# A hybrid decoder step: the first feed-forward slice by four plain products, tiles turned in another order

## The chip, the cores and the metric

The kernel runs on one core of one Trainium2 chip. The metric is device time in microseconds (us) of one execution. The engines are PE (TensorE matmuls), ACT (ScalarE), DVE (VectorE), POOL (GpSimd) and SP, which issues most DMAs.

## What is computed

One layer of a decoder for 1024 prompt tokens and 64 sample tokens (8 sequences of 8), all in float32:

```python
h = h + concat([o_gla, o_mla]) @ w_o                # (1024+64) x 1024
n = rmsnorm(h, g_ffn)
a, c = n @ ffn_w_gate, n @ ffn_w_up                 # 1024 -> 2816 each
conv = b + sum(w[j] * full[:, j:j + T] for j in range(3))   # causal, full = prev + a
h = h + (silu(conv) * c) @ ffn_w_down
h = h + (p @ ple_w_proj) * sigmoid(rmsnorm(h, g_ple) @ ple_w_gate)
```

`o_gla` is gated linear attention, `o_mla` multi-head latent attention; for the sample tokens the latter goes over a paged cache of 8192 past positions for each sequence.

## The kernel before, in words

Every float32 operand of a matmul is split into a high part (a cast on ACT) and a low part (the difference, on DVE or POOL; `split`, lines 114 to 117). A product is three matmuls: high by high, high by low, low by high (`mm3`, lines 138 to 141). The compiler's list scheduler orders the instructions of each engine; the program's text gives the priority, `keep_in_program_order` and `issue_after` hold single instructions back. `issue_after(x)` sets the instructions of its block that run on x's engine behind x. Engines then run their queues in order.

**Stages.** Dense projections and prompt attention run first, together with the cache stream: 64 blocks of the paged cache (`cache_stream`), each scored, softmaxed (`stage_b`, `stage_c1`) and multiplied (`stage_pv`, L646). When the dense work has ended, the stream runs on with the output projection as filler: `wo_units` is a generator of 65 units, of which unit 1 loads operands. Six passes over channel pairs make units 2 to 49; the last 16 units (channels 6 and 7) go tile by tile, two halves of 512 columns for each 128-row tile, in the order `order = (6, 7, 0, 3, 1, 4, 2, 5)`. Each adds its PSUM result to the residual rows (L1441). When a tile has both halves, `normed` makes its row sums (L1467 on ACT, L1468 and L1469 on POOL), copies the rows to DRAM (L1599), and normalises them in place (`xnorm`): by one DVE operation (L1476), or, for the tiles whose bit is set in `VIAP`, by ACT and then POOL (L1478, L1479). VIAP = 20 picks tiles 2 and 4. `fill(n)` draws n units; the last blocks of the stream draw 1, 3, 2, 1, 5 and 4.

**Hand-over.** Then come, in the text's order: tiles 6 and 7 turned for the "rest" (`turned_rest`: 8 transpositions, L132, and two splits each), three calls of `turned_pair`, the sample rows' share of `w_o` (`down_sample`, with weights `w45` of channels 4 and 5 loaded through the staging rooms `stg`, of which there are three), and `normed` and `turned_rest` of the sample rows.

**Slices.** The feed-forward goes in 22 slices of 128 columns (`ff_chunk`). Tokens 0 to 767 are two halves of NP = 384 columns, inputs are two halves of 512 features, so gate and up of a slice are a 2 by 2 block product. It is made with seven products (Winograd's form): with input blocks 11, 21 (tokens 0 to 383) and 12, 22 (tokens 384 to 767), `turned_pair(t)` turns tiles t and t + 3 and forms

```python
t1 = x12 - x11;  t2 = x22 - t1;  t3 = t2 - x11;  t4 = x21 - t2
```

in the rooms of the rows themselves (`quarter`), and splits 11, 21, 22, t1 to t4 (`put`). `ff_weights(f)` loads four weight blocks g0, g1, u0, u1 (L1713), forms four sums s1 to s4 on POOL (L1720 to L1726) and splits eight blocks into a ring of rooms (`wroom`, NWB = 10: four in pool `fw`, six in `fv`). A product is 12 matmuls of 384 columns. The remaining 256 prompt and 64 sample columns (NR = 320) are the "rest": 24 plain matmuls for gate and 24 for up. Slice 0 does its gate rest late, behind the turned sample rows; the others do it after the first two products.

**Rooms.** SBUF pools are opened on two sides like stacks; a room opened where another was waits, tile by tile, for the last use of what lay there. Decode constants and block rooms are in `cp` on the right. `wo_room` lays out on the left, in turn, `hp` (the eight row tiles, 6 and 7 first, and the gain), `wq`, `fb`, `wf`, `ct`, `sg`. After the stream, `xhl` (turned blocks) takes the right side, then `xh2`, `fw`, `fv`; `tp` (slice buffers) takes the left side.

**PSUM.** There are eight banks: pools pd (3), pm (2), and, after the stream, p2t (2) and p2 (1). `both` deals them out in turn to the products.

After the slices come the down projection, the per-layer embedding and the outputs.

Of the kernel before, what the change touches and what calls it, by code (L numbers as in the profile page):

```python
# [18 lines left out]
P = 128  # L19
D = 1024  # L20
# [9 lines left out]
PLAN = ([0], [], [1, 2, 3])  # L30
VIAP = 20
GS0 = 1
# [12 lines left out]
def step_kernel(ctx: ExitStack, tc: tile.TileContext, A):  # L45
# [561 lines left out]
    def stage_c1(o):  # L607

        nt = o.nt
        sb = o.sn[:, :nt, :]  # L610
        mt = pm([P, 512], "mt")
        drain = o.n - NB * 8 + 3
        if drain == 1:
            fill(49 - z["units"])
        elif drain == 2:
            fill(2)
        pe.transpose(mt[:, 0:P], o.ml.rearrange("p a c -> p (a c)"), ident)
        m = cp.tile([P, 1], F32, tag="bm", name="bm", bufs=4)
# [11 lines left out]
        act.copy(phl[:, :nt, 0:64], sb)  # L630
        pool.tensor_tensor(phl[:, :nt, 64:128], sb, phl[:, :nt, 0:64].bitcast(F32), ALU.subtract)  # L631
# [25 lines left out]
    def stage_c2(o):  # L657
# [14 lines left out]
        dve.tensor_scalar(ol, ol, rl, None, ALU.mult)  # L672
        if b == NB - 1:
            fill(4)
        pt = pm([P, 512], "pt_ol")
# [847 lines left out]
    room = {}  # L1523
    order = (6, 7, 0, 3, 1, 4, 2, 5)

    def wo_room():
# [5 lines left out]
        z["late"], z["WvT"] = (z["fb"].tile([P, n], F32, name=nm) for nm, n in (("late", 648), ("WvT", 512)))  # L1532
        room["wf"] = opened("wf", 2)
        room["ct"] = opened("ct")
        room["sg"] = opened("sg")

    def wo_units():
# [3 lines left out]
        for g in range(3):  # L1541
# [98 lines left out]

    tw = opened("tw")
    w45 = [wload(z["tw"], A["w_o"][0][c * P:(c + 1) * P, :], 1, D, "w45", 2, 3, stg) for c in (4, 5)]

    NP = 384
    NR = T - 2 * NP + R
    rx = opened("xhl", side="right")  # L1650
    xb = {nm: [z["xhl"].tile([P, 4, NP], F32R, name=f"x{nm}{s}") for s in "hl"] for nm in ("t2", "t1", "22", "21", "11")}
    xr = [z["xhl"].tile([P, 8, NR], F32R, name=f"xr{s}") for s in "hl"]

    def turned_rest(t):
# [9 lines left out]

    def turned_pair(t):

        pt = {}
        for nm, bank, rows, k0 in (("11", p2t, t, 0), ("12", pd, t + 3, 0), ("22", pd, t + 3, 4), ("21", p2t, t, 4)):
            pt[nm] = bank([P, 4, P], "pt")
            for k in range(4):  # L1670
                pe.transpose(pt[nm][:, k], hrows(rows)[:, (k0 + k) * P:(k0 + k + 1) * P], ident)
        b11, t1, t2, t3 = quarter(t, 0), quarter(t, 1), quarter(t + 3, 0), quarter(t + 3, 1)
        act.copy(b11, pt["11"])
        dve.tensor_tensor(t1, pt["12"], b11, ALU.subtract)
        dve.tensor_tensor(t2, pt["22"], t1, ALU.subtract)
# [3 lines left out]
        pool.tensor_tensor(t3, t2, b11, ALU.subtract)
# [15 lines left out]
    def wroom():  # L1695

        i = ring[0] % NWB
        ring[0] += 1
        where, n = (z["fw"], 4) if i < 4 else (z["fv"], NWB - 4)
        return [where.tile([P, 4, P], F32R, tag="w" + s, name="w" + s, bufs=n) for s in "hl"]  # L1700
# [60 lines left out]
    def ff_chunk(f):  # L1761
# [105 lines left out]
    for t in range(3):
        turned_pair(t)
    for f in range(2):
        down_sample([(z["oTm"][:, c], [w[:, 0, f * 512:f * 512 + 512] for w in w45[c]]) for c in (0, 1)] +  # L1870
                    [(z["oTm"][:, c - 4], wow[c, f]) for c in (6, 7)], pm, f, f == 0)
# [3 lines left out]
    rx2 = opened("xh2", side="right")
    xb.update({nm: [z["xh2"].tile([P, 4, NP], F32R, name=f"x{nm}{s}") for s in "hl"] for nm in ("t4", "t3")})
    for t in range(3):
        last_sums(t)
    normed(NT)
    room["hp"].close()  # L1880
# [9 lines left out]
    rt.close()  # L1890
    fv.close()
    fw.close()
    rx2.close()
    rx.close()

# [367 lines left out]
```

## Time and profile before

| what | value |
|---|---|
| runs, us | 2217.87, 2218.1, 2211.19 (median 2217.87) |
| span of the profiled execution, us | 2211.1 |
| PE busy, us (matmuls) | 2126.7 (13460) |
| DVE busy, us | 1668.4 |
| ACT busy, us | 1366.7 |
| POOL busy, us | 1233.9 |
| mean granted clock of PE | 0.988 |

The span runs from the first to the last instruction of one execution; the runs are timed by themselves and lie between 0.1 and 7.0 us above it. In a line of the order in time, the columns are start, duration, engine, source line, operation, what it writes and reads, shape and number of merged instructions; in brackets stands the idle time ahead of it and what ended it. In a list of groups, busy time and mean duration in ns follow the count. "L139" is line 139 of the program, often one of a helper, so the tile's name tells more.

### The profile page before, as it was taken

How to read it: one execution, taken by the hardware profiler on the slowest of the kernel's cores; microseconds unless marked ns; L12 is line 12 of the kernel's file. 1: busy time of each engine (PE TensorE's matmuls, PEld its weight loads, DVE VectorE, ACT ScalarE, POOL GpSimd, SP SyncE). 2: the span in 40 equal slices, each digit the busy share in tenths (PEclk: the TensorE clock that was granted, in tenths of full speed). 3: DMA queues.
4: the chain of work that ended last, by engine and by line, in shares of the span. 5: the costliest groups of instructions: out<-in, count | busy, mean ns of one | idle time of the engine just before them, and what ended most of it. 6: DMA issues, size and time to landing. Idle time of an engine off the chain costs nothing.

```text
span 2211.1 us, 38379 instructions
## 1 busy us (share of the span) xinstructions
PE 2126.7 (96%) x13460; PEld 1927.2 (87%) x13460; DVE 1668.4 (75%) x2551; ACT 1366.7 (62%) x3724; POOL 1233.9 (56%) x1330
## 2 busy tenths in 40 slices
PE   7999989999999999999999997999999999999999
PEld 6889978878888888887898875999999999888899
DVE  4775667467788888887888788888888886887642
ACT  5676766777778888887777766333333333534631
POOL 5675668576777777778455557756566562011100
PEclk9999999999999999999999998999999999999999
DMA  5343235412342222221522222332232325777321
GB/s 185 106 144 108 78 119 156 141 54 69 105 120 61 63 74 61 61 56 46 171 77 69 74 77 82 101 102 90 92 95 91 101 91 191 240 218 237 101 71 39
DMA packets 204418, 233.07 MB, mean 105 GB/s; under 512 B 42422, under 2 KB 146339, under 8 KB 204227
## 3 DMA queue, kind: packets, MB, share of 16 engines
q1 hardware_dynamic: 188259, 179.49, 26.0%
q0 software_dynamic: 14736, 46.67, 7.4%
q10 hardware_dynamic: 1232, 4.46, 0.5%
q8 instruction: 108, 1.77, 0.3%
q14 instruction: 83, 0.68, 0.1%
HBM read 188.00 MB, written 42.52 MB: 104 GB/s over the span
## 4 chain that ended last, share of the span: by engine, by line
PE 79%; DVE 7%; ACT 5%; DMA 3%; POOL 3%; issue 2%; SPq 0%; DVEq 0%; POOLq 0%; ACTq 0%
PE ps_gu L140 7%; PE ps_gu L141 7%; PE ps_gu L139 7%; PE ks L139 5%; PE ks L141 4%; PE ks L140 4%; PE ps_dn L140 3%; PE ps_dn L141 3%; PE ps_dn L139 3%; PE cpv L646 2%; PE ctp L522 2%; PE ps_lt L278 2%; PE ps_pj L139 2%; DVE css L565 1%; PE ps_pj L140 1%
## 5 line engine op out<-in xcount | busy, mean ns | idle before, releaser
L560 ACT ACTIVATE csq<-ks 128x256 f32<-128x256 f32 x1040 | 392.7, 400 | 91.1 <-PE ks L141 80.2
L565 DVE TENSOR_REDUCE css<-csq 128x16 f32<-128x1024 f32 (+1 forms) x264 | 315.7, 1196 | 61.2 <-ACT csq L560 58.2
L115 ACT CAST wh<-st 128x512 fp32r<-128x512 f32 x176 | 108.4, 619 | 189.0 <-PE ps_gu L140 168.7
L139 PE MATMUL ks<-mv0h,cTh 128*128 128x320 f32 (+1 forms) x520 | 171.0, 331 | 8.8 <-ACT sn L562 4.6
L139 PE MATMUL ks<-mv1h,cTh 128*128 128x320 f32 (+1 forms) x520 | 169.6, 328 | 7.8 <-ACT sn L562 3.5
L605 POOL TENSOR_TENSOR chl<-craw,chl 128x1024 fp32r<-128x1024 f32 x64 | 141.6, 2213 | 55.2 <-ACT chl L603 53.0
L140 PE MATMUL ks<-mv1l,cTh 128*128 128x320 f32 (+1 forms) x520 | 153.1, 296 | 0.0
L140 PE MATMUL ks<-mv0l,cTh 128*128 128x320 f32 (+1 forms) x520 | 152.0, 294 | 0.0
L141 PE MATMUL ks<-mv0h,cTl 128*128 128x320 f32 (+1 forms) x520 | 147.6, 297 | 0.9 <-DVE cTl L116 0.8
L141 PE MATMUL ks<-mv1h,cTl 128*128 128x320 f32 (+1 forms) x520 | 148.0, 298 | 0.1
L116 DVE TENSOR_TENSOR wl<-st,wh 128x512 fp32r<-128x512 f32 x132 | 119.0, 903 | 26.3 <-ACT wh L115 26.3
L631 POOL TENSOR_TENSOR phl<-sn,phl 128x512 fp32r<-128x512 f32 (+1 forms) x64 | 85.5, 1335 | 84.8 <-ACT phl L630 84.3
L116 POOL TENSOR_TENSOR wl<-st,wh 128x512 fp32r<-128x512 f32 x44 | 69.4, 1578 | 102.9 <-ACT wh L115 102.9
L140 PE MATMUL ps_dn<-o 128*128 128x512 f32 x308 | 120.1, 390 | 0.4 <-DVE o L116 0.4
L141 PE MATMUL ps_dn<-o 128*128 128x512 f32 x308 | 120.2, 390 | 0.0
L116 DVE TENSOR_TENSOR cTl<-ctp,cTh 128x512 fp32r<-128x512 f32 (+1 forms) x136 | 90.0, 662 | 37.8 <-ACT cTh L115 36.8
L139 PEld LDWEIGHTS ks<-mv0h,cTh 128*128 128x128 f32 x520 | 97.9, 188 | 23.2 <-ACT sn L562 9.4
L562 ACT COPY sn<-ks 128x64 f32<-128x64 f32 x520 | 116.7, 224 | 0.0
L139 PEld LDWEIGHTS ks<-mv1h,cTh 128*128 128x128 f32 x520 | 99.0, 190 | 20.1 <-ACT sn L562 7.9
L1318 POOL TENSOR_TENSOR pl<-p,ph 128x512 fp32r<-128x512 f32 (+1 forms) x96 | 97.5, 1020 | 30.3 <-DVE ph L1317 21.2
L139 PE MATMUL ps_dn<-o 128*128 128x512 f32 x308 | 112.1, 390 | 0.0
L141 PE MATMUL ps_gu<-xrh,wl 128*128 128x320 f32 x352 | 108.7, 309 | 0.0
(670 smaller groups left out, 7871.4 us busy)
## 6 DMA issues: line engine op xcount, KB each, us to landing
raw<-ds SPq DMA_DIRECT2D x77, 256.0 KB
raw<-ffn_w_down SPq DMA_DIRECT2D x66, 256.0 KB
stage<-w_in SPq DMA_DIRECT2D x48, 256.0 KB
st<-ffn_w_gate SPq DMA_DIRECT2D x44, 256.0 KB
st<-ffn_w_up SPq DMA_DIRECT2D x44, 256.0 KB
wr<-ffn_w_down SPq DMA_DIRECT2D x44, 256.0 KB
ds<-cv SPq DMA_DIRECT2D x21, 512.0 KB
oraw<-doT SPq DMA_DIRECT2D x16, 256.0 KB
```

What stands on the lines that cost most here:

```text
L115: cast = act.copy(hi, src)
L116: res = (lo_eng or dve).tensor_tensor(lo, src, hi.bitcast(F32), ALU.subtract)
L139: pe.matmul(ps, ah, bh, start=first, stop=False)
L140: pe.matmul(ps, ah, bl, start=False, stop=False)
L141: return pe.matmul(ps, al, bh, start=False, stop=last)
L278: pe.matmul(ps, x, w, start=first, stop=last)
L560: act.activation(sq[:, f * 256:f * 256 + 256], ks[:, 0:256], AF.Square)
L562: act.copy(o.sn[:, g0 + i, :], ks[:, 256:320])
L565: dve.tensor_reduce(o.ss[:, g0 + i + 1 - n:g0 + i + 1, :].rearrange("p i h -> p (i h)"), sq2[:, :n].rearrange("p i (h n) -> p (i h) n", n= ...
L605: pool.tensor_tensor(ch[:, c0:c1, 128:256], src, ch[:, c0:c1, 0:128].bitcast(F32), ALU.subtract)
L631: pool.tensor_tensor(phl[:, :nt, 64:128], sb, phl[:, :nt, 0:64].bitcast(F32), ALU.subtract)
L1318: pool.tensor_tensor(pl[:, c0:], p[:, c0:], ph[:, c0:].bitcast(F32), ALU.subtract)
```

## The change

The first slice is computed by four plain products of 24 matmuls each (`plain`: gate and up for both halves of tokens), which need blocks 11, 21, 12, 22 and the four plain weight blocks only. Its elementwise part is a function of its own (`first_chunk`). The weights of slice 0 are loaded and split through the staging rooms `stg` with `ff_weights(0)`, whose ACT casts are set behind the last block's softmax cast (`z["phl"]`), into a new pool `fr` on the right side. The last 16 projection units go in tile order 0 to 7; the last four of them are no longer drawn by the stream's last block (`fill(4)` is gone) but drawn among the calls that turn tiles 0 to 5 (`turned_tile`). The sums t1 and t2 still come from turning, t3, t4 and the splits of t1 to t4 in `sums` and a `put` around the last plain products. VIAP = 85 picks tiles 0, 2, 4 and 6 for ACT and POOL. Rows are laid as 6, 7, 3, 4, 5, 0, 1, 2, `sg` below `ct`, `ct` is closed before `xhl`, and `tp`'s rooms in another order. The `w45` weights go to rooms of `wf` in place of a pool of their own. Slices 1 to 21 are computed as before.

```diff
-VIAP = 20
+VIAP = 85
...
-        act.copy(phl[:, :nt, 0:64], sb)
+        z["phl"] = act.copy(phl[:, :nt, 0:64], sb)
...
-        if b == NB - 1:
-            fill(4)
...
-    order = (6, 7, 0, 3, 1, 4, 2, 5)
+    order = (6, 7, 3, 4, 5, 0, 1, 2)
...
-        for t in order:
+        for t in range(NT):
             for f in range(2):
                 wo_unit((6, 7), t, f)
...
-    def turned_pair(t):
+    def turned_tile(t):
+        n, rest = t % 3, t > 2
+        raw = []
+        for i, nm in enumerate(("12", "22") if rest else ("11", "21")):
+            pt = (pd, p2t)[i]([P, 4, P], "pt")
             for k in range(4):
+                pe.transpose(pt[:, k], hrows(t)[:, (4 * i + k) * P:(4 * i + k + 1) * P], ident)
+            put(n, nm, pt, dve)
+            raw.append(pt)
+        b11, b21 = quarter(n, 0), quarter(n, 1)
+        if not rest:
+            act.copy(b11, raw[0])
+            act.copy(b21, raw[1])
+        else:
+            t1, t2 = quarter(t, 0), quarter(t, 1)
+            dve.tensor_tensor(t1, raw[0], b11, ALU.subtract)
+            dve.tensor_tensor(t2, raw[1], t1, ALU.subtract)
+    def sums(n):
+        b11, b21, t1, t2 = quarter(n, 0), quarter(n, 1), quarter(n + 3, 0), quarter(n + 3, 1)
+        put(n, "t2", t2, dve)
+        pool.tensor_tensor(b11, t2, b11, ALU.subtract)
+        put(n, "t1", t1, pool)
+        pool.tensor_tensor(b21, b21, t2, ALU.subtract)
+        put(n, "t3", b11, pool)
...
+    def plain(key, ws, xs):
+        ps = early[key] = both([P, 512], "ps_gu")
+        for i, (wn, xn) in enumerate(zip(ws, xs)):
+            for k in range(4):
+                mm3(ps[:, :NP], wgu[0][wn][0][:, k], wgu[0][wn][1][:, k], xb[xn][0][:, k], xb[xn][1][:, k],
+                    i == k == 0, i == 1 and k == 3)
...
+    unit = lambda: next(z["fill"], done) is None
+    with tc.issue_after(z["phl"].ins):
+        ff_weights(0)
+    for w in (0, 1, unit, 2, unit, unit, 3, unit, 4, 5):
+        w() if w is unit else turned_tile(w)
...
+    plain("g1", ("g0", "g1"), ("11", "21"))
+    for f in range(2):
+        down_sample([(z["oTm"][:, c - 4], wow[c, f]) for c in (6, 7)] +
+                    [(z["oTm"][:, c], w45[2 * c + f]) for c in (0, 1)], pm, f, f == 0)
+    plain("u1", ("u0", "u1"), ("11", "21"))
     turned_rest(6)
     turned_rest(7)
...
+    normed(NT)
+    plain("g2", ("g0", "g1"), ("12", "22"))
+    for n in range(3):
+        sums(n)
+    plain("u2", ("u0", "u1"), ("12", "22"))
...
+    for n in range(3):
+        put(n, "t4", quarter(n, 1), dve)
+    turned_rest(NT)
```

More of the change, by code (lines that the diff above doesn't have):

```diff
@@ L1533, in wo_room @@
         room["wf"] = opened("wf", 2)
+        room["sg"] = opened("sg")
         room["ct"] = opened("ct")
-        room["sg"] = opened("sg")
     def wo_units():
@@ L1639, in both @@
         return (pd, pm, pd, pm, pd, p2)[turn[0]](shape, name)
-    tw = opened("tw")
-    w45 = [wload(z["tw"], A["w_o"][0][c * P:(c + 1) * P, :], 1, D, "w45", 2, 3, stg) for c in (4, 5)]
     NP = 384
     NR = T - 2 * NP + R
+    room["ct"].close()
     rx = opened("xhl", side="right")
-    xb = {nm: [z["xhl"].tile([P, 4, NP], F32R, name=f"x{nm}{s}") for s in "hl"] for nm in ("t2", "t1", "22", "21", "11")}
+    xb = {nm: [z["xhl"].tile([P, 4, NP], F32R, tag=f"x{nm}{s}", name=f"x{nm}{s}") for s in "hl"]
+          for nm in ("t2", "22", "11", "21", "t1", "12")}
     xr = [z["xhl"].tile([P, 8, NR], F32R, name=f"xr{s}") for s in "hl"]
+    fr = opened("fr", side="right")
     def turned_rest(t):
@@ L1698, in wroom @@
         ring[0] += 1
-        where, n = (z["fw"], 4) if i < 4 else (z["fv"], NWB - 4)
+        where, n = (z["fr"], 4) if i < 4 else (z["fv"], NWB - 4)
         return [where.tile([P, 4, P], F32R, tag="w" + s, name="w" + s, bufs=n) for s in "hl"]
@@ L1708, in ff_weights @@
         fs = slice(f * P, (f + 1) * P)
-        raw, hl = [], wroom()
+        raw, hl = [], wroom() if f else None
         for nm in ("ffn_w_gate", "ffn_w_up"):
             for i in range(2):
-                r = wstage()
+                r = wstage() if f else stg([P, 512], F32).rearrange("p (k c) -> p k c", c=P)
                 sp.dma_start(r, A[nm][0][i * 512:(i + 1) * 512, fs].rearrange("(k p) c -> p k c", p=P))
                 raw.append(r)
+        w = wgu[f] = {}
+        if not f:
+            for nm, r, eng in zip(("g0", "g1", "u0", "u1"), raw, (pool, pool, dve, dve)):
+                w[nm] = block(r, eng)
+            return
         g0, g1, u0, u1 = raw
         s1, s2 = wstage(), wstage()
-        w = wgu[f] = {}
         w["g0"] = block(g0, dve, hl)
@@ L1782, in ff_chunk @@
         pool.tensor_copy(a_s[:, :, 0:2], prv[:, f])
+        if not f:
+            return first_chunk(w, a, a_s, cv, cvs, conv, w3)
         m1, m2 = product("g0", "11"), product("g1", "21")
@@ L1791, in gate_rest @@
             act.copy(a_s[:, :, 2:10], pg[:, T - 2 * NP:NR].rearrange("p (b t) -> p b t", t=8))
-        if f:
-            gate_rest()
+        gate_rest()
         if f + 1 < NF:
@@ L1847, in ff_chunk @@
         dve.tensor_tensor(v, m4, v, ALU.add)
-        if not f:
-            turned_rest(NT)
-            gate_rest()
         if not last:
@@ new lines, in step_kernel @@
+    unit = lambda: next(z["fill"], done) is None
[3 more added lines that the diff above has]
+        w() if w is unit else turned_tile(w)
+    for _ in z["fill"]:
+        raise AssertionError
+    w45 = []
+    for c in (4, 5):
+        for f in range(2):
+            hl = [z["wf"].tile([P, 512], F32R, tag=f"s{f}{k}", name=f"s{k}", bufs=2) for k in "hl"]
+            raw = stg([P, 512], F32)
+            sp.dma_start(raw, A["w_o"][0][c * P:(c + 1) * P, f * 512:f * 512 + 512])
+            split(*hl, raw)
+            w45.append(hl)
@@ L1865, in step_kernel @@
+    plain("g1", ("g0", "g1"), ("11", "21"))
+    for f in range(2):
+        down_sample([(z["oTm"][:, c - 4], wow[c, f]) for c in (6, 7)] +
+                    [(z["oTm"][:, c], w45[2 * c + f]) for c in (0, 1)], pm, f, f == 0)
+    plain("u1", ("u0", "u1"), ("11", "21"))
     turned_rest(6)
     turned_rest(7)
[L1867 to L1871, printed above, removed]
@@ L1872, in step_kernel @@
-    tw.close()
-    for nm in ("sg", "ct", "wf", "fb", "wq"):
-        room[nm].close()
[L1875 to L1880, printed above, removed]
+    room["sg"].close()
+    room["wf"].close()
+    rx2 = opened("xh2", side="right")
+    xb["t3"] = [z["xh2"].tile([P, 4, NP], F32R, name=f"xt3{s}") for s in "hl"]
+    normed(NT)
@@ L1889, in step_kernel @@
         sample_rows(late[0], half)
[L1890 to L1894, printed above, removed]
+    for r in (rt, fv, fw, rx2, fr, rx):
+        r.close()
     NK = NF // 2
```

53 lines of the change are left out of this document (32 added, 21 removed).

## The prediction

> **What bounds the kernel now.** I read the page first, then the busy time by stage, then who waited for whom, and last the matmuls in order of time across the hand-over from the decode stream to the feed-forward slices.
>
> ```profile
> span 2211.1 us, 38379 instructions
> ```
> ```profile
> 1300.20:1323.30 23.10, 21.54 (x108) 17.36 (x107) 19.39 (x29) 13.72 (x34) 15.94 (x19) 1.00 0.28 114
> 1323.30:1359.89 36.59, 22.34 (x115) 16.64 (x114) 31.84 (x47) 27.23 (x56) 25.73 (x20) 0.83 0.28 87
> 1359.89:1395.67 35.78, 33.58 (x189) 31.50 (x189) 29.86 (x35) 15.88 (x30) 28.96 (x26) 0.93 0.32 89
> 1395.67:1860.00 464.33, 464.33 (x2799) 460.65 (x2798) 388.31 (x519) 177.16 (x348) 272.19 (x261) 1.00 0.29 95
> ```
>
> The columns are length, then busy time of PE, PEld, DVE, ACT and POOL, then granted clock. From 1395.67 to the end of the slices PE is busy all the time at full clock. So whatever brings the matmul stream forward before 1395.67 shortens the kernel by as much, and nothing behind that point changes. The loss sits in 1323.30 to 1359.89, where PE is busy 22 of 37 us and even that at a clock of 0.83.
>
> ```profile
> PE ps_gu L139 <- ACT wh L115: 6.4, 1, 6.4
> PE pt L1671 <- DVE h L1674: 2.3, 2, 1.7
> PE pt L1671 <- DVE x22l L116: 2.1, 1, 2.1
> ```
>
> The first slice's matmuls wait 6.4 us for its weight cast on ScalarE; the transpositions of paired tiles (L1671) wait again and again for the subtraction that frees a PSUM bank.
>
> **The matmul ledger of before.** I take the stretch from the first matmul of the last four projection units to the point at which slice 0 is finished and slice 1 has done its two gate products and its gate rest.
>
> ```profile
> 1313.90 1.03 PE L132 MATMUL pt<-ident,h 128*128 128x128 f32 x8
> 1323.30 0.39 PE L1434 MATMUL ps_dn<-wdh,sh 128*128 128x512 f32 x1
> 1328.65 0.39 PE L1438 MATMUL ps_dn<-wdh,sl 128*128 128x512 f32 x1
> 1333.02 1.15 PE L717 MATMUL po_mla<-oTm,WvT 128*64 128x64 f32 x16
> 1351.49 0.39 PE L1447 MATMUL ps_ds<-w45h,oTm 128*128 128x512 f32 x1
> 1353.11 0.39 PE L1450 MATMUL ps_ds<-wdl,oTm 128*128 128x512 f32 x1
> 1359.89 0.69 PE L139 MATMUL ps_gu<-x11h,wh 128*128 128x384 f32 x1 [6.39 <-ACT wh L115]
> 1362.51 0.52 PE L139 MATMUL ps_gu<-x11h,wh 128*128 128x384 f32 x1
> 1364.75 0.39 PE L140 MATMUL ps_gu<-x11l,wh 128*128 128x384 f32 x1
> 1376.47 0.33 PE L139 MATMUL ps_gu<-xt4h,wh 128*128 128x384 f32 x1
> 1378.38 0.34 PE L141 MATMUL ps_gu<-xt4h,wl 128*128 128x384 f32 x1
> 1378.65 0.71 PE L132 MATMUL pt<-ident,hs 64*128 64x64 f32 x8
> 1380.46 0.41 PE L139 MATMUL ps_gu<-x21h,wh 128*128 128x384 f32 x1 [1.10 <-DVE a L1811]
> 1393.03 0.31 PE L139 MATMUL ps_gu<-xrh,wh 128*128 128x320 f32 x1
> 1395.52 0.31 PE L141 MATMUL ps_gu<-xrh,wl 128*128 128x320 f32 x1
> 1395.67 0.34 PE L139 MATMUL ps_gu<-xt2h,wh 128*128 128x384 f32 x1
> ```
>
> Matmuls overlap, so the price of one is the distance between starts. 24 projection matmuls from 1323.30 to 1328.65: 5.35/23 = 0.2326 us. 8 sample matmuls from 1351.49 to 1353.11: 1.62/7 = 0.231. Twelve products of 384 columns from 1376.47 to 1378.38: 1.91/11 = 0.1736. Eighteen of 320 columns from 1393.03 to 1395.52: 2.49/17 = 0.1465. Work between 1323.30 and 1395.67:
> 24 projection 5.6; seven tiles to turn, 7 x 1.03 = 7.2 (the eighth, tile 6, was turned in the gap at 1313.90); sample rows 0.7; the decode output 1.2; 16 sample matmuls 3.7; slice 0: seven products of 12, 84 x 0.1736 = 14.6, and two rests of 24, 48 x 0.1465 = 7.0; slice 1: 24 x 0.1736 = 4.2 and 24 x 0.1465 = 3.5. Sum 47.7. The stretch lasts 1395.67 - 1323.30 = 72.4, so 24.7 us are lost.
>
> **The change, part by part.** *Plain products.* Slice 0 takes four products of 24 matmuls in place of seven of 12: 96 for 84, 12 x 0.1736 = 2.1 us more on PE, all on the path. In return nothing of t1 to t4 and no s1 to s4 is needed before PE may start slice 0.
> *Turning.* Eight turned tiles as before; 7.2 to 8.2 us in the stretch, by whether the gap at 1313.90 takes tile 0. I take 7.7. PE work after: 47.7 + 2.1 + 0.5 = 50.3. With no loss at all the gain is 72.4 - 50.3 = 22.1 us.
> *Tile order and normalisation.* Tiles go 0 to 7, and VIAP moves tiles 0, 2, 4, 6 to ScalarE and GpSimd where only 2 and 4 were.
>
> ```profile
> L1476 DVE SCALAR_TENSOR_TENSOR h<-h,rs,gb 128x1024 f32<-128x1024 f32 x6 | 8.7, 1451 | 1.5 <-DMA dhp<-h 1.5
> L1479 POOL TENSOR_TENSOR h<-h,gb 128x1024 f32<-128x1024 f32 x2 | 4.7, 2364 | 3.5 <-ACT h L1478 3.5
> L1478 ACT ACTIVATE h<-h,rs 128x1024 f32<-128x1024 f32 x2 | 2.3, 1151 | 0.2 <-POOL rs L1469 0.2
> 1318.54 1.30 POOL L631 TENSOR_TENSOR phl<-sn,phl 128x512 fp32r<-128x512 f32 x1 [1.91 <-ACT phl L630]
> 1322.33 1.12 PE L646 MATMUL cpv<-chl,phl 128*128 128x258 f32 x8
> ```
>
> DVE sheds 2 x 1.45, ACT gains 2 x 1.15, POOL gains 2 x 2.36. On POOL one such norm may now stand ahead of the last softmax split (L631). That ends at 1319.84 and its matmuls start at 1322.33, behind projection units: a slack of 2.5 us covers a norm of 2.36. I cost it at 0; without the cover, 2.4.
> *Weights of slice 0.* Their casts go right behind the last softmax cast on ACT, with three staging rooms.
>
> ```profile
> 1282.81 5.34 SPq L157 DMA_DIRECT2D stg<-w_o  x3
> 1326.76 0.33 SPq L157 DMA_DIRECT2D stg<-w_o  x1
> 1373.29 3.76 DMA st<-ffn_w_up
> ```
>
> Before, the same three rooms took three w_o loads at 1282.81, 44 us before the fourth, which got its room at 1326.76. In the new order the weights of slice 0 stand in those places: three lie ready, the fourth lands at about 1326.8 + 3.8 = 1331. So the 6.4 us wait goes. What is late next is the turned tiles.
>
> *Loss 1, the tiles.* These are the rows for the vector work:
>
> ```profile
> L1441 DVE TENSOR_TENSOR h<-h,ps_dn 128x512 f32<-128x512 f32 x16 | 10.7, 679 | 3.0 <-PE ps_dn L1438 3.0
> L116 DVE TENSOR_TENSOR x21l<-pt,x21h 128x512 fp32r<-128x512 f32 x3 | 2.0, 677 | 0.0
> L116 DVE TENSOR_TENSOR xt4l<-h,xt4h 128x512 fp32r<-128x512 f32 x3 | 4.7, 1620 | 0.4 <-ACT xt4h L115 0.4
> L116 POOL TENSOR_TENSOR xt3l<-h,xt3h 128x512 fp32r<-128x512 f32 x3 | 4.6, 1571 | 2.7 <-ACT xt3h L115 2.7
> L1679 POOL TENSOR_TENSOR h<-h,h 128x512 f32<-128x512 f32 x3 | 4.2, 1390 | 0.9 <-DVE h L1675 0.9
> 1336.74 1.29 DVE L1476 SCALAR_TENSOR_TENSOR h<-h,rs,gb 128x1024 f32<-128x1024 f32 x1 [1.52 <-DMA dhp<-h]
> ```
>
> From 1323.30 DVE still has 4 additions of 0.68, one norm of 1.45, 6 splits of tiles 0 to 2 and 12 operations of tiles 3 to 5 at 0.68, and the low halves of u0 and u1 at 0.68: 2.7 + 1.45 + 4.1 + 8.2 + 1.4 = 17.9, to 1341. Two tiles turned earlier take off 2.7, and the first product needs tile 5's banks, not its last subtractions, another 1.4 or more: 1336 to 1340. PE's own work before its first plain product is 5.6 + 1.2 + 5 or 6 tiles, so 1335 to 1336. I take 3.5 lost; 1 if DVE keeps up, 8 if every norm waits for the copy of its row to DRAM as at 1336.74.
> *Loss 2, the clock.* At 1362.51 to 1364.75 the products ran 2.24/7 = 0.32 us apart, not 0.1736, after the idle stretch. The new stretch has shorter gaps: 1 us, bounds 0 and 2.4 (as before: 16 products slow by 0.146).
> *Loss 3, slice 1.* Its staging rooms open behind those of the projection and the rows; a load costs 3.76 to land, then GpSimd's four subtractions of 1.39 and the splits. PE has the sample matmuls, u1, g2, u2 and two rests meanwhile. 2 us, bounds 0 and 6.
> *Loss 4, sample rows.* They need both sample sums, a row norm and a turn before the rests, as at 1380.46 (1.10 idle). 1 us, bounds 0 and 3.
> The sums t1 to t4 leave the way to slice 0 and get some 20 us of PE work as cover; uncovered they would cost rival B.
> Losses 7.5, so the gain is 22.1 - 7.5 = 14.6 us, with bounds 22.1 - 1 = 21.1 and 22.1 - 19.4 = 2.7. The page's span of 2211.1 is 6.8 below the median of the three runs, 2217.87, and 0.1 below the lowest. The gain is in matmul time behind no transfer, so I take it from the median: 2217.87 - 14.6 = 2203.3. About 0.3%, 6.7 us, is what a measurement of this kernel can tell from no change.
>
> **Rivals.** *A: DVE is held up by GpSimd.* The xt4l splits, both inputs in SBUF and an xt3l split running on POOL, took 1.62 each where the split from PSUM took 0.68. After the change four w_o splits, two of u, six of the sums and three norms have two SBUF inputs, and POOL runs sums and norms beside them: 15 x 0.94 = 14.1 at worst, and DVE was already busy 31.8 of 36.6 us. With half of it on the path, 7: gain 7.6, 2210.3. Against: the splits on the way to the first product read PSUM.
> [...]
> *B: POOL becomes the bound.* The sums are 6 subtractions of 1.39 and 6 splits of 1.57 on POOL, 17.8 us, and tile 6's norm 2.4 before them: from 1341 to 1361. Slice 1's four subtractions (5.6) end at 1367 if they follow at once, and by the forecast PE wants s2 and t2 at 1323.30 + 50.3 + 7.5 = 1381.1. If the sums run behind g2, as the program's text has them, POOL starts at about 1353 and ends at 1379, and the splits follow: some 6 us late. Gain 8.6, 2209.3.
> *C: slower, the staging rooms.* Eight loads, four of the slice and four of w_o, share three rooms; five must wait for a split, 1.57 on POOL, and a landing, 3.76. Should each cast stand at the head of ACT's queue while it waits, the row sums, tile copies and scales behind it stand too: 5 x 5.3 = 26.6. Then 14.6 - 26.6 = -12.0, 2229.9. It decides from 14.6 + 6.7 = 21.3 us of such standing, four of the five. Against: three loads should lie ready 44 us ahead, and the sample sums are not wanted until after g1.
> *D: the start does not move.* If rooms of the decode stream come free only with its last result, tiles and weights start together after 1332, and the first plain product stays near 1350; with 2.1 more on PE and the sums free, gain 0 to 6: 2214.9.
>
> **Numbers.** Forecast 0.50, A 0.16, B 0.16, C 0.10, D 0.08. Faster: 0.48 of the forecast, 0.06 of A, 0.12 of B, 0.01 of D: 0.67. Same: 0.02 + 0.09 + 0.04 + 0.06 + 0.01 = 0.22. Slower: 0.11. The likeliest case alone spans 2196.8 to 2210; the range goes to 2195 below, and above to 2218, past A, B and D, which leaves out C and little else.
>
> **What would show it.** Right: the first plain product between 1335 and 1342; slice 1's first t2 product near 1381, not 1395.7; 96 matmuls of slice 0 in four groups; granted clock of 0.9 or more from 1323 to 1360; no wait of ps_gu for a weight cast over 2 us; PE at 100% from there, as before. Loss 1 is wrong if transpositions wait over 8 us together, loss 3 if slice 1's products wait for POOL or a DMA. A shows as splits of 1.6 us on DVE filling its time, B as PE waiting for xt splits, C as ACT idle behind a DMA. The prediction fails if anything ahead of 1300 moves, since I hold all of that equal although rooms of the rows are laid in another order.
> [...]

## The result, and the profile after

The changed kernel takes 2222.49 us (median of 20 runs, 2217.29 to 2226.22) against 2217.23 for the kernel before (20 runs beside them): ratio 1.0025, 95% interval 1.0017 to 1.0033. It is slower by about 5 us, where 14.6 us of gain were forecast. The profiled execution took 2221.21 us, 1.8 above its span.

The first view is the page's first line, then the busy time by stage (length, busy PE, PEld, DVE, ACT, POOL, granted clock; the last two columns are DMA's share and GB/s):

```profile
span 2219.4 us, 38390 instructions
```
```profile
1300.20:1324.55 24.35, 22.79 (x117) 18.46 (x117) 18.68 (x28) 17.75 (x42) 20.65 (x19) 1.00 0.27 108
1324.55:1342.70 18.15, 13.10 (x69) 10.04 (x67) 14.16 (x22) 12.26 (x27) 9.28 (x10) 0.81 0.36 131
1342.70:1362.65 19.95, 19.24 (x112) 17.37 (x110) 18.21 (x24) 12.05 (x23) 16.14 (x11) 1.00 0.11 39
1362.65:1400.00 37.35, 28.11 (x149) 26.57 (x149) 29.94 (x39) 18.43 (x38) 23.59 (x26) 0.87 0.30 86
1400.00:1860.00 460.00, 460.00 (x2766) 456.44 (x2766) 388.70 (x509) 172.63 (x341) 269.51 (x257) 1.00 0.29 93
```

The start did move: the first plain product comes at 1342.70, 17 us earlier than the 1359.89 of before. The third row shows PE nearly full. The fourth row is new: from 1362.65 PE is busy 28 of 37 us at a clock of 0.87. The first view below says who ended PE's idle time (1300 to 1402), the second has PE's own rows:

```profile
PE pt L132 <- DVE hs L1474: 3.4, 1, 3.4
PE ps_gu L139 <- DVE a L1792: 2.2, 1, 2.2
PE ps_gu L139 <- ACT xt3h L115: 2.2, 1, 2.2
PE pt L1667 <- DVE h L1439: 2.0, 1, 2.0
PE pt L1667 <- ACT h L1673: 1.7, 1, 1.7
PE ps_gu L140 <- DVE xrl L116: 1.5, 1, 1.5
```
```profile
1333.65 0.77 PE L1432 MATMUL ps_dn<-wdh,sh 128*128 128x512 f32 x1
1338.48 0.52 PE L1436 MATMUL ps_dn<-wdh,sl 128*128 128x512 f32 x1
1342.70 0.43 PE L139 MATMUL ps_gu<-x11h,wh 128*128 128x384 f32 x1
1360.55 0.47 PE L1445 MATMUL ps_ds<-wdh,oTm 128*128 128x512 f32 x1 [0.36 <-DVE hs L1456]
1366.03 0.63 PE L139 MATMUL ps_gu<-x12h,wh 128*128 128x384 f32 x1 [2.17 <-ACT xt3h L115]
1366.46 0.53 PE L140 MATMUL ps_gu<-x12l,wh 128*128 128x384 f32 x1
1366.78 0.53 PE L141 MATMUL ps_gu<-x12h,wl 128*128 128x384 f32 x1
1375.45 0.68 PE L132 MATMUL pt<-ident,hs 64*128 64x64 f32 x8 [3.44 <-DVE hs L1474]
1397.05 0.69 PE L139 MATMUL ps_gu<-xt2h,wh 128*128 128x384 f32 x1 [2.17 <-DVE a L1792]
1865.95 0.40 PE L1763 MATMUL ps_ds<-wdl,ssm 128*128 128x512 f32 x1
1869.86 1.19 PE L139 MATMUL ps_dn<-o 128*128 128x512 f32 x4 [3.51 <-ACT o L115]
```

Three things are to be seen. Between 1360 and 1376 PE waits for the sample rows: the second half of their sum starts only at 1360.55, the second gate product behind it at 1366.03, the transpositions of hs at 1375.45, the last two with products 0.32 us apart for a while instead of 0.17. (xt3h is no operand of the second gate product; what ended at 1365.89 is the fold of the second half, L1456, which frees the bank.) Then PE waits 2.17 us ahead of slice 1's first t2 product at 1397.05, for an addition (L1792) that stands late in DVE's queue. And 500 us later, where the forecast held everything equal, PE waits 3.5 us before the down projection.

For all comparisons below I divide each trace at two marks: the last ks matmul of the decode stream, and the last ps_ds matmul of the slices. **Stretch A** lies between them, **stretch B** from there to the end. What lies ahead of the first mark differs by run and not by kernel: it ends between 1300.1 and 1311.0 in the traces, but the median times less A and B leave 1303 to 1307 us for every kernel, the one before and the changed ones (about 2 us of it is what a run's time lies above its span).

| kernel | A | B | A + B against before | ratio of the times (95%) |
|---|---|---|---|---|
| before | 562.29 | 348.38 |  |  |
| changed | 564.55 | 353.45 | +7.3 | 1.0025 (1.0017 to 1.0033) |
| x loads later on SP | 564.49 | 348.07 | +1.9 | 1.0008 (0.9998 to 1.0018) |
| sample sums in two banks | 559.92 | 352.51 | +1.8 | 1.0008 (0.9999 to 1.0017) |
| norm before t4 on DVE | 561.02 | 353.20 | +3.6 | 1.0017 (1.0007 to 1.0028) |
| VIAP 20 | 564.24 | 352.84 | +6.4 | 1.0039 (1.0025 to 1.0052) |
| rs first on POOL | 559.34 | 353.16 | +1.8 | 1.0008 (0.9999 to 1.0017) |
| no wait for sample rows | 559.46 | 353.89 | +2.7 | 0.9997 (0.9986 to 1.0008) |
| x loads, rs first | 560.58 | 348.14 | -2.0 | 0.9988 (0.9979 to 0.9997) |
| x loads, banks, rs first | 560.68 | 348.07 | -1.9 | 0.9984 (0.9975 to 0.9993) |
| T: these three, t4 behind xrl | 560.86 | 348.10 | -1.7 | 0.9982 (0.9972 to 0.9992) |
| T, sample norm on ACT and POOL | 563.42 | 348.09 | +0.8 | 1.0002 (0.9992 to 1.0012) |
| T, xt3 split on DVE | 560.03 | 348.07 | -2.6 | 0.9991 (0.9982 to 1.0000) |
| T, xt3 split on DVE, sample rows ahead | 557.61 | 348.13 | -4.9 | 0.9973 (0.9964 to 0.9982) |
| T, POOL's sums left out | 554.27 | 348.10 | -8.3 | 0.9958 (0.9944 to 0.9971) |

0.001 is 2.2 us. The traces' column and the ratios agree within 3.4 us, most within 2. Each row of A and B is one trace; the runs "rs first on POOL" and "x loads, rs first" have the same order on DVE and POOL in this stage and differ by 1.2 us in A (the clock, see below), so differences in A of less than about 1.5 us prove nothing. So the change lost 2.3 us in A, where it was to gain 14.6, and 5.1 in B.

### The profile page after: what moved, and what is told of

Same layout as the page of the kernel before. It is cut to its first block, busy times and chain, and to the rows that moved or that the text cites. A ratio compares the mean times of both kernels' runs of the same rounds, so it can differ in the third digit from the quotient of the medians.

```text
span 2219.4 us, 38390 instructions
## 1 busy us (share of the span) xinstructions
PE 2134.2 (96%) x13472; PEld 1934.3 (87%) x13472; DVE 1670.8 (75%) x2544; ACT 1366.8 (62%) x3728; POOL 1227.6 (55%) x1326
## 4 chain that ended last, share of the span: by engine, by line
PE 79%; DVE 8%; ACT 5%; DMA 3%; POOL 3%; issue 2%; SPq 0%; DVEq 0%; ACTq 0%; POOLq 0%
PE ps_gu L140 7%; PE ps_gu L139 7%; PE ps_gu L141 7%; PE ks L139 5%; PE ks L141 4%; PE ks L140 4%; PE ps_dn L141 3%; PE ps_dn L140 3%; PE ps_dn L139 3%; PE cpv L646 2%; PE ctp L522 2%; PE ps_lt L278 2%; PE ps_pj L139 2%; PE ps_pj L140 1%; PE ps_pj L141 1%
## 5 line engine op out<-in xcount | busy, mean ns | idle before, releaser
L115 ACT CAST wh<-st 128x512 fp32r<-128x512 f32 x168 | 103.4, 618 | 174.8 <-PE ps_gu L140 159.1
L116 DVE TENSOR_TENSOR wl<-st,wh 128x512 fp32r<-128x512 f32 x126 | 112.8, 897 | 28.2 <-ACT wh L115 28.2
L140 PE MATMUL ps_gu<-xrl,wh 128*128 128x320 f32 x352 | 108.4, 308 | 1.5 <-DVE xrl L116 1.5
```

The lines of the kernel that those rows point to most:

```text
L115: cast = act.copy(hi, src)
L116: res = (lo_eng or dve).tensor_tensor(lo, src, hi.bitcast(F32), ALU.subtract)
L140: pe.matmul(ps, ah, bl, start=False, stop=False)
```

## The experiments

**B: a queue 500 us away.** The first fence has SP's queue (its last column counts the loads) and ACT in the changed kernel at the start of the down projection, the second the same place before.

```profile
1854.22 0.33 SPq L1754 DMA_DIRECT2D wr<-ffn_w_down  x1
1854.64 9.04 SPq L2022 DMA_DIRECT2D raw<-ds  x3
1863.74 0.42 SPq L2017 DMA_DIRECT2D st<-ds  x1
...
1868.76 1.04 ACT L115 CAST o<-st 128x1024 fp32r<-128x1024 f32 x1 [6.68 <-DMA st<-ffn_w_down]
```
```profile
1851.98 0.34 SPq L1960 DMA_DIRECT2D st<-ds  x1
...
1858.74 3.08 ACT L115 CAST o<-st 128x1024 fp32r<-128x1024 f32 x3
```

Three loads for a later product (`x` of product 5, L2022) now stand ahead of the first loads of product 1 and hold SP for 9 us. The diff touches neither line; the scheduler laid SP's order anew, and why it came out this way stays open.

```diff
-        sp.dma_start(r[:, 1], cols_of(*b, k))
+        col = sp.dma_start(r[:, 1], cols_of(*b, k))
+        if p == 1:
+            z["st_in"] = col.ins
...
-            sp.dma_start(x, rows_of(1, 0, k))
+            with tc.issue_after(z["st_in"]):
+                sp.dma_start(x, rows_of(1, 0, k))
```

> Edit to the changed kernel: the loads of product 5's third operand (raw<-ds, x3) are queued on SP behind the last column load of product 1, as in the kernel before, in place of ahead of product 1's first loads (st<-ds). Nothing else. Theory (queue order): 5.1 us of the loss lies at the start of the down projection, where PE waits 3.5 us for ScalarE's cast of the first st rows and then runs 8 matmuls at half speed, because those rows stand on SP behind a raw load that has to wait for its room. Then the time falls by 4 to 5.5 us, from 1.0025 to about 1.0002 of the kernel before (2217 to 2218.5 us), and PE's wait for o at the first ps_dn falls below 0.5 us. Rival (the rows themselves are late, or product 5 then waits in its turn): the wait moves to product 5 or stays; within 1.5 us of the changed kernel's 2222.5.

The last sample sum and the first product of the down projection in this run:

```profile
1872.23 0.39 PE L1763 MATMUL ps_ds<-wdl,ssm 128*128 128x512 f32 x1
1872.46 1.08 PE L139 MATMUL ps_dn<-o 128*128 128x512 f32 x4
```

The wait is gone, B is 348.1 as before (348.4), and A is unchanged. The time fell by 0.0017, 3.8 us (2217.66 median), just under the 4 to 5.5 of the theory; B fell by 5.4. The theory holds: all that the change lost in B is this order.

**A second trace of the kernel before.**

> The kernel before once more, for a second trace of it. Theory (what lies ahead of the seam differs by run, not by kernel): the last ks matmul, at 1300.4 in the first trace of it and at 1301.4 in that of the changed kernel, lies between 1300 and 1308 as in the four experiments so far; the stretches behind it repeat within 0.5 us: 59.5 to the first product of slice 0, 35.8 from there to slice 1's first t2 product, 348.4 from the last sample sum to the end. Rival (the new rooms and tile order cost time ahead of the seam): it stays at 1300.4 within 0.5.

The marks repeat: 59.5 from the last ks matmul to the first product, 36.0 (35.8) from there to slice 1's first t2 product, 348.3 at the end. The mark itself lay at 1301.18, which alone decides nothing; the medians above do.

**A: three edits to the sample rows' chain.** The sums of the 64 sample rows are made in two halves, folded into hs on DVE, squared on ACT, scaled by two small POOL operations (ss, rs), normed on DVE, turned on PE. First, a bank for each half:

```diff
-                    [(z["oTm"][:, c], w45[2 * c + f]) for c in (0, 1)], pm, f, f == 0)
+                    [(z["oTm"][:, c], w45[2 * c + f]) for c in (0, 1)], (pm, p2)[f], f, f == 0)
```

> Edit to the changed kernel: the two halves of the last sample sum (ps_ds) take one PSUM bank each, the second one another than the first, in place of one after the other in the bank that slice 0's first gate product leaves. Theory (bank chain): the second half no longer waits until 1360.5 for the fold of the first, it is done at about 1353; the second plain gate product starts right behind the up product, at about 1361 and without the 2.2 us of idleness and the 1.5 us of slow clock behind it; the sample rows' norm comes 2 to 4 us earlier. Together 3 to 6 us: 2216.5 to 2219.5 us, 0.9997 to 1.0012 of the kernel before. Rival (VectorE is the bound: it is idle 0.2 us between 1344 and 1363): the folds come no sooner, the waits move behind the second gate product onto the sample rows' norm, and the time moves by less than 1.5 us.

```profile
1366.73 0.41 PE L139 MATMUL ps_gu<-x12h,wh 128*128 128x384 f32 x1 [0.54 <-DVE hs L1456]
...
1380.77 1.08 PE L132 MATMUL pt<-ident,hs 64*128 64x64 f32 x8 [5.62 <-DVE hs L1474]
```

Half of each theory: the idle 2.17 ahead of the second gate product shrank to 0.54 and A fell by 4.6, but the wait for hs grew from 3.44 to 5.62, as the rival said. Next, the norm ahead of the t4 splits:

```diff
...
-    for n in range(3):
-        put(n, "t4", quarter(n, 1), dve)
+    with tc.issue_after(z["normed"]):
+        for n in range(3):
+            put(n, "t4", quarter(n, 1), dve)
```

> Edit to the changed kernel: VectorE makes the sample rows' norm before the three t4 splits, which stood ahead of it. Theory (order on VectorE): the sample rows' transpositions start 2 to 3 us earlier than 1375.45, the 3.4 us wait of PE falls below 1.5, and 2 to 4 us are won: 2218.5 to 2220.5 us. Rival (slice 1's weights are the real end of the chain: their rooms lie over the rows that the t4 splits read): the casts of slice 1's weights come 1.3 us later than 1374.19, PE waits for them instead, and the time stays within 1 us of 2222.5.

A fell by 3.5, the time by 0.0008, 1.8 us. PE still waited 3.1 us for hs, where the theory had less than 1.5, since DVE now waited 4.65 us for rs. That led to POOL's queue. In the changed kernel the squares are made at 1365.98, and then:

```profile
1365.08 3.73 POOL L116 TENSOR_TENSOR xt3l<-h,xt3h 128x512 fp32r<-128x512 f32 x3 [0.93 <-ACT xt3h L115]
1368.90 0.29 POOL L1466 TENSOR_SCALAR ss<-ss 64x1 f32<-64x1 f32 x1
1369.27 1.28 POOL L1724 TENSOR_TENSOR st<-st 128x512 f32<-128x512 f32 x1
1370.51 0.56 POOL L1467 TENSOR_TENSOR rs<-ss,mhalf 64x1 f32<-64x1 f32 x1
```

Two operations on 64 numbers stand behind three splits and a subtraction. So they were put first:

```diff
...
-        put(n, "t3", b11, pool)
+        with tc.issue_after(z["rs_i"]):
+            put(n, "t3", b11, pool)
...
-        pool.tensor_tensor(s1, u0, u1, ALU.add)
+        with tc.issue_after(z["rs_i"]) if f == 1 else nullcontext():
+            pool.tensor_tensor(s1, u0, u1, ALU.add)
```

> Edit to the changed kernel: the two small GpSimd operations of the sample rows' norm (ss, 64x1, and rs, 64x1) go ahead of the three xt3 splits and of slice 1's first subtraction, behind which they stood. Theory (two small operations in a long queue): hs is whole at 1365.9 and its squares at 1366.7, but rs comes at 1371.1 and the norm at 1374.0; with the new order rs is done at about 1367.7 and the norm before 1370, while PE is in the second gate product until 1371.8. The 3.4 us wait of PE for hs and most of the slow clock behind it go: 3.5 to 5 us won, ratio to the kernel before 1.0002 to 1.0009 (after: 1.0025). Rival (slice 1's weights are as late: their casts start at 1374.2 and their rooms wait for the t4 splits): PE waits there instead, under 2 us won, ratio above 1.0016.

A fell by 5.2, the time by 3.8 us, as much as the theory gave. And a bound on what the chain costs, slices that take no sample rows (the sums, folds and norm are still made):

```diff
-    turned_rest(NT)
+    transpose_split(p2t, hrows(7)[:R], R, lambda c0: tuple(x[:, c0:c0 + 4, 2 * P:2 * P + R] for x in xr), True)
```

> The changed kernel with one part of the computation replaced: in the feed-forward slices the sample rows are taken from tile 7's first 64 rows, so that no matmul of the slices waits for the sample sums, their folds and their norm (all of which are still made). It bounds what the sample rows' chain costs at this place. Theory: PE's 3.4 us wait for hs and the slow clock behind it are all that the chain costs directly, the bank chain stays: 4 to 6 us won, ratio 1.0000 to 1.0008, like the order of GpSimd's queue alone. Rival (slice 1's weights): under 2 us, since PE then waits for the casts that start at 1374.2.

A is 559.5, 5.1 below the changed kernel and equal to the order of POOL's queue alone; by the time it is 6 us (0.0028). So the wait for hs, with the slow clock behind it, is worth about 5, and what else is lost in A lies elsewhere.

**VIAP 20 again.**

> Edit to the changed kernel: only tiles 2 and 4 are normalised on ScalarE and GpSimd, as in the kernel before; 0 and 6 go back to VectorE. Rival theory A of the prediction (GpSimd and VectorE hold each other up): two norms of 3.4 us beside 2.3 to 2.8 us splits go, the first plain product starts 2 us or more earlier than 1342.7, and 2 to 4 us are won. Theory (what follows is bound by the sample sums, whatever the first product does): the first product moves by at most 2 us either way, and the time stays within 1.5 us of 2222.5.

The first plain product came 42.9 us behind the last ks matmul, not earlier than the 41.3 of the changed kernel. A is the same within 0.3; the time is 0.0014 more, with intervals that overlap. So taking two norms from POOL wins nothing. It does not refute rival A, since the norms go back to DVE as operations with two SBUF operands (L1474, 1.27 to 1.87 us each in the changed kernel).

**Do the three edits add up?** All three together, and the first with the third:

> The changed kernel with three edits together: product 5's third operand queued later on SP (alone: 3.8 us won by the ratio, 5.3 us by the traces' last stretch), the two halves of the sample sum in banks of their own (alone: 3.8), and the sample norm's two GpSimd operations ahead of the xt3 splits. Theory (three separate causes): they add up, less what the second and the third have in common: 9 to 13 us under the changed kernel, 0.9965 to 0.9985 of the kernel before, faster than both. Rival (they stand in one chain, with VectorE full behind all of them): not more than 6 us, 0.9998 or above.

> The changed kernel with two edits: product 5's third operand later on SP, and the sample norm's two GpSimd operations ahead of the xt3 splits (not the banks). Theory (the two causes lie 500 us apart and add up): in the traces each took 5.2 us off its stretch; both together 9 to 11 us under the changed kernel, 0.9975 to 0.9985 of the kernel before, as fast as or faster than with the banks as well, since those gave nothing on top. Rival (the stretches trade with one another): above 0.9995.

Both are faster than the kernel before, at 0.9984 and 0.9988; the first lies in its expected range, the second just above. B adds on in full. But in A the gains do not add up: 560.7 with all three and 560.6 without the banks, where the order of POOL's queue alone had 559.3. The banks, worth 4.6 alone, give nothing on top. The trace says what took their gain: PE waits 6.7 us for the sample norm, on DVE. Here it is in the run with all three, and below it POOL from rs on:

```profile
1369.43 5.82 DVE L1474 SCALAR_TENSOR_TENSOR hs<-hs,rs,gb 64x1024 f32<-64x1024 f32 x1 [1.27 <-DMA dhs<-hs]
```
```profile
1367.44 0.56 POOL L1467 TENSOR_TENSOR rs<-ss,mhalf 64x1 f32<-64x1 f32 x1
1367.97 2.54 POOL L116 TENSOR_TENSOR xt3l<-h,xt3h 128x512 fp32r<-128x512 f32 x2
1370.47 1.26 POOL L1726 TENSOR_TENSOR st<-st 128x512 f32<-128x512 f32 x1
1371.70 1.25 POOL L116 TENSOR_TENSOR xt3l<-h,xt3h 128x512 fp32r<-128x512 f32 x1
1372.92 1.25 POOL L1727 TENSOR_TENSOR st<-st 128x512 f32<-128x512 f32 x1
1374.12 0.09 POOL L1787 MEMSET a<- 128x2 f32 x1
```

The norm took 1.27 us in the changed kernel (1374.04), where POOL was idle or busy with small things. Here it ends at 1375.25, 1.1 us behind the last of five POOL operations that follow each other without a gap. Is it the order of DVE's queue, or POOL? First the splits of tiles 6 and 7 (xrl) ahead of those of t4:

```diff
...
+    whole = z["turned"]
...
-    for n in range(3):
-        put(n, "t4", quarter(n, 1), dve)
+    with tc.issue_after(whole):
+        for n in range(3):
+            put(n, "t4", quarter(n, 1), dve)
```

> The run with all three edits, and besides the t4 splits on VectorE behind the splits of tiles 6 and 7 (xrl), which stood behind them. Theory (VectorE is held by GpSimd): in that run the sample norm, 1.27 us by itself, took 5.82 us on VectorE and ended 1.1 us behind the last of a row of GpSimd operations without a gap; the order of the splits behind it changes nothing on that, the norm again takes over 4 us, and the 6.7 us wait of PE becomes one of 4 us or more; 0.9975 to 0.9988 of the kernel before. Rival (the order of the splits was the cause): the wait falls below 2 us, 0.9965 or less.

```profile
1365.92 5.92 DVE L1474 SCALAR_TENSOR_TENSOR hs<-hs,rs,gb 64x1024 f32<-64x1024 f32 x1 [1.18 <-DMA dhs<-hs]
1371.77 1.27 DVE L116 TENSOR_TENSOR xrl<-pt,xrh 128x512 fp32r<-128x512 f32 x2
```

The norm takes 5.92, PE waits 4.8, A is 560.9: not the order. Then the norm off DVE (VIAP = 341, whose bit 8 is the sample rows; the xt3 splits and slice 1's first subtraction behind it):

> As the one with the splits set behind, but the sample norm is made on ScalarE (scale) and GpSimd (gain) in place of VectorE, ahead of the xt3 splits. Theory (VectorE held by GpSimd): with no operation of VectorE between the sample sums and the transpositions of hs that reads two SBUF operands, hs is normed some 3.5 to 4 us behind its rs (1.1 and 2.4), not 7; PE's wait falls by 2 to 5 us, 0.9955 to 0.9975 of the kernel before. Rival (GpSimd is the bound): its 2.4 us more come back as later xt3 splits and slice 1's subtractions, PE waits for these, no gain over the run with all three edits, 0.9980 or more.

```profile
1372.40 3.71 POOL L116 TENSOR_TENSOR xt3l<-h,xt3h 128x512 fp32r<-128x512 f32 x3
1376.09 1.70 POOL L1726 TENSOR_TENSOR st<-st 128x512 f32<-128x512 f32 x1
```
```profile
1373.28 7.08 DVE L116 TENSOR_TENSOR xt4l<-h,xt4h 128x512 fp32r<-128x512 f32 x3
```

The theory's number failed (1.0002, A 563.4), and the rival's held (0.9980 or more). But PE did not wait for POOL, as the rival had it: it waited 6.4 us for the sample rows' xrl on DVE. With the norm gone, the next operations of DVE with two SBUF operands, three splits, stand beside POOL's row (now with the norm in it) and take 7.08 us, and xrl stands behind them. Then the xt3 splits off POOL and onto DVE, behind t4:

```diff
...
-        put(n, "t3", b11, pool)
...
+    with tc.issue_after(whole):
+        for nm, f in (("t4", 1), ("t3", 0)):
+            for n in range(3):
+                put(n, nm, quarter(n, f), dve)
```

> As the run with all three edits and the xrl splits set ahead, but the low halves of xt3 are made on VectorE, behind those of xt4, in place of GpSimd. No work is left out and VectorE gets three splits more. Theory (VectorE's operations with two SBUF operands are held for as long as GpSimd's queue has no gap): behind rs GpSimd has two subtractions of 1.26 us and then small operations, in place of six operations in a row; the sample norm, 5.82 and 5.92 us before, takes 1.3 to 3 us, the xt4 and xt3 splits 0.6 to 0.7 us each, and PE's wait of 4.8 us falls to 2 or less: 0.9960 to 0.9975 of the kernel before, against 0.9982. Rival (VectorE's own load counts): three more splits of 0.6 to 1.6 us push back the splits of the sample rows and of slice 1's weights; the norm is as long as before or the wait only moves; 0.9980 or more.

```profile
1367.72 2.36 DVE L1474 SCALAR_TENSOR_TENSOR hs<-hs,rs,gb 64x1024 f32<-64x1024 f32 x1 [1.18 <-POOL st L1724]
1370.01 1.27 DVE L116 TENSOR_TENSOR xrl<-pt,xrh 128x512 fp32r<-128x512 f32 x2
1371.21 1.88 DVE L116 TENSOR_TENSOR xt4l<-h,xt4h 128x512 fp32r<-128x512 f32 x3
1373.01 1.88 DVE L116 TENSOR_TENSOR xt3l<-h,xt3h 128x512 fp32r<-128x512 f32 x3
```

Every duration came as the theory had it (2.36, and 0.63 for a split), but the time did not: 0.9991, not separable from 0.9982, as the rival had it. PE now waited 3.0 us for the sample rows' xrl, which stood behind the six splits: DVE's own load counts too. Two runs settled the rest. The first takes POOL's work away:

```diff
-        pool.tensor_tensor(b11, t2, b11, ALU.subtract)
-        put(n, "t1", t1, pool)
-        pool.tensor_tensor(b21, b21, t2, ALU.subtract)
-        put(n, "t3", b11, pool)
+        for s_ in xb["t1"]:
+            act.copy(s_[:, :, n * P:(n + 1) * P], t1)
...
+            for s_ in xb["t3"]:
+                act.copy(s_[:, :, n * P:(n + 1) * P], b11)
```

> The run with all three edits and the xrl splits set ahead, with part of the computation left out: GpSimd makes neither the two subtractions of the row sums (six of 128x512) nor the low halves of xt1 and xt3 (six more); both halves are written by plain copies on ScalarE, which has room. So GpSimd is nearly idle beside slice 0, while VectorE and TensorE have the same work. Theory (VectorE, full from the first plain product on, loses time to GpSimd): the sample norm falls from 5.9 us to 1.3 to 2.6, the three xt2 splits from 4.7 to 2, the two folds from 2.9 to 1.4; 4 to 7 of these 8 us are on PE's path: the stretch from the last ks matmul to the last sample sum falls from 560.9 to 554 to 557, ratio 0.9950 to 0.9965. Rival (VectorE's own operations and slice 1's weights are the bound, what GpSimd does hardly counts): 559 or more, ratio 0.9975 to 0.9985.

The same stage of DVE, first in the changed kernel, then in this run:

```profile
1352.55 1.78 DVE L116 TENSOR_TENSOR xt2l<-h,xt2h 128x512 fp32r<-128x512 f32 x1
1356.64 1.46 DVE L1455 TENSOR_TENSOR hs<-hs,fd 64x512 f32<-64x512 f32 x1
1360.32 1.44 DVE L116 TENSOR_TENSOR xt2l<-h,xt2h 128x512 fp32r<-128x512 f32 x1
```
```profile
1356.49 0.68 DVE L116 TENSOR_TENSOR xt2l<-h,xt2h 128x512 fp32r<-128x512 f32 x1
1359.48 0.67 DVE L1455 TENSOR_TENSOR hs<-hs,fd 64x512 f32<-64x512 f32 x1
1362.48 0.68 DVE L116 TENSOR_TENSOR xt2l<-h,xt2h 128x512 fp32r<-128x512 f32 x1
```

Splits and folds take 0.67 to 0.68 each instead of 1.2 to 1.8 (1.16 to 1.78 in the run that this one is built on), A falls from 560.9 to 554.3 and the ratio from 0.9982 to 0.9958. DVE's queue has the same order in both runs, and in the run with POOL's work neither PE nor DVE waits for a result of POOL in this stage. So POOL's work beside slice 0 costs 6.6 us on PE's path (5.3 by the ratios), through DVE's longer operations. ACT makes six copies more here, which, if anything, hides a part. The second run leaves nothing out and puts the sample rows' splits ahead of the six:

```diff
...
-    with tc.issue_after(whole):
+    turned_rest(NT)
+    with tc.issue_after(z["turned"]):
         for nm, f in (("t4", 1), ("t3", 0)):
             for n in range(3):
                 put(n, nm, quarter(n, f), dve)
-    turned_rest(NT)
```

> As the run with the xt3 splits on VectorE, but the sample rows' splits stand ahead of the six splits of xt4 and xt3. Nothing is left out. Theory (order of VectorE's queue): PE's wait of 3.0 us for the sample rows' xrl goes, the casts of slice 1's weights come about 0.7 us later; 2 to 3 us won: 0.9970 to 0.9982 of the kernel before, the stretch from the last ks matmul to the last sample sum 557 to 558.5. Rival (slice 1's weights come next): PE waits for these, the stretch stays within 1 us of 560.0.

A is 557.6 and the ratio 0.9973 (0.9964 to 0.9982), 2210.01 us against 2215.69 beside it. This version, the changed kernel with five small edits (x loads, banks, rs first, xt3 on DVE, the sample rows' splits ahead), beats both kernels: by 6 us the one before and, by the two ratios, by some 11 the changed one.

## Why the prediction was wrong, point by point

*"Nothing behind that point changes"* failed. PE was 100% busy through the slices, before and after, and I took that as proof that a gain there is handed on whole. It says nothing of the next stage: SP's queue was laid anew and cost 5.1 us in B, which one edit gave back.

*The work* (2.1 for 12 more matmuls, turning) holds: 1.5 tiles were turned in the earlier gaps where I reckoned between nothing and one, so PE's work in the hand-over is 49.3, not 50.3. Without any loss A would have been 562.3 - 72.4 + 49.3 = 539.2. It was 564.55: 25.4 lost, as much as the 24.7 of before, where 7.5 were forecast.

*Losses 1 and 2* (4.5, bounds 1 to 10.4) were 8.5 ahead of the first product. The hand-over starts 22.87 behind the last ks matmul, 1324.27 here; PE had 24 projection matmuls 5.6, the decode output 1.2 and 24 transpositions 3.1 to do, 9.9 of the 18.4 us to 1342.70. PE's waits there are 5.1 us (0.63, 1.96, 0.77, 1.69), inside the bounds of loss 1. The granted clock was 0.81 there, where I had asked for 0.9. The first product itself lies 0.7 behind the window of 1335 to 1342, no more than the run's later start (1.0).

*Loss 2, the clock,* is a term that failed: 1 us, at most 2.4, an estimate from shorter gaps that no run shows. The twelve projection matmuls from 1333.65 to 1338.48 are 0.43 us apart in place of 0.2326, which is 2.3 us. Behind the first product three stretches of some ten products 0.32 apart, from 1366.03, 1376.06 and 1397.05, cost 1.5 to 1.7 each. That is 7.0 in all.

*Losses 3 and 4* are the other terms that failed: 3 us forecast with a bound of 9, measured 25.4 - 8.5 = 16.9. By the changed kernel's own trace, 9.9 of these are waits of PE (0.32, 0.36, 2.17, 3.44, 1.45, 2.17), all but one given as ended by DVE and that one, as said above, by a fold on DVE; 4.7 are the slow clock behind them. I had written that PE "has the sample matmuls, u1, g2, u2 and two rests meanwhile" and never laid out DVE's queue behind the first product, as I had done ahead of it. The runs split the 16.9: 3.7 (564.55 to 560.86) go with the banks and the order of POOL's and DVE's queues, 6.6 with POOL's work beside DVE, and 6.6 are left in the run without it. That run's trace still has PE waits of 0.46, 1.64, 0.37 and 0.98 us and one stretch at the slow clock (ten products of 320 columns 0.27 apart in place of 0.1465, 1.2 us); the other 2 us are not taken apart. Since stretches at the slow clock (1.2 to 1.7 us each) came behind some waits and not behind others, each of these three parts is good to some 1.5 us.

*The clock.* I had counted on the shorter gaps to cost little, which was an estimate. Behind 2.17 us of idleness ahead of the second gate product the products ran 0.32 apart (1366.46 to 1366.78 in the rows above), and so they did behind the 3.44 at 1375.45 (1376.36 to 1379.30); behind the 3.51 at 1869.86 products of 512 columns ran 0.43 apart (1871.62 to 1873.76) in place of the 0.23 of the same products in the run "x loads later on SP" (1873.94 to 1874.87). The length of the waits alone does not decide it: with nearly the same waits (1.90, 0.21, 0.62 in the run "rs first on POOL", 1.96, 0.21, 0.61 in "x loads, rs first") the products of 320 columns behind them ran 0.147 apart in the first run and, for twelve of them, 0.27 apart in the second. That is 1.5 us, about the 1.2 by which the two differ in A.

*Rival A* was the mechanism, with the wrong place. I held against it that the splits on the way to the first product read PSUM. That is so for the tiles, but two weight splits between them read SBUF twice and took 2.28 and 2.81 us (1323.01 and 1332.52) where I had put 0.68; whether PE paid for these is not shown. Behind the first product the first fold of each half (L1455), the norm and the xt2 and xt4 splits read SBUF twice. Its price of 7 us is close to the 6.6 measured. The folds and the xt2 splits took 1.2 to 1.8 us beside POOL's work against 0.67 to 0.68 without it, and the norm's 5.82 lasted over five POOL operations. The rival's times, 2210.3 with half of its 14.1 us on the path and 2217.4 with all (a gain of 14.6 - 14.1 = 0.5), were both nearer than the forecast. That 2217.4 came so near is in part luck: it held neither the clock's 7 us nor the order of the queues nor B.

*Rival B* is not what happened: POOL had rs late, but PE waited for DVE, and xt3 was done by 1368.8. *Rival C* did not come: no wait of ps_gu for a weight cast is left among PE's waits. *Rival D* fell with the first product 17 us earlier. The signs I named did their work: 96 matmuls in four groups, yes; slice 1's first t2 product near 1381, no, 1397.05.

## What to carry to other kernels

When a start is moved forward, lay out the queue of every engine up to the next full stage, not only up to the first matmul: the gain ended here where the slowest queue stood, VectorE's. Work given to GpSimd was not free beside VectorE operations with two SBUF operands (6.6 us in A here); look for VectorE rows that are far above their own best (here 1.45 against 0.67, and 5.82 against 1.27), and for small GpSimd operations that someone waits for behind bulk (here rs, 5.2 us in A). And compare the order of the DMA queues in stages that the diff does not touch.

## What the runs showed of the hardware

In two runs a DVE operation with two SBUF operands ended 1.1 us behind the last of five POOL operations that followed each other without a gap: the sample norm, 1.27 us in the changed kernel, took 5.82 ("x loads, banks, rs first") and 5.92 (T), the POOL operations 1.25 to 1.27 each. Three splits beside the row of POOL operations in "T, sample norm on ACT and POOL" took 7.08 us in place of 1.88 (T, xt4). Where DVE's own operations followed each other as closely (1352 to 1361 in the changed kernel), both took longer: splits and folds 1.2 to 1.8 us in place of 0.67, and POOL's subtraction at 1351.51 in the changed kernel 2.27 in place of 1.26 (1362.89).
